# A separate tile for the first output rows, and a recut of a transformer block's head: loads, scalings, the turn of the weight splits

## The chip, the cores and the metric

The kernel runs on one core of one Trainium2 chip. A core has a matrix engine (PE, with its weight loads as PEld), three engines that work on rows (DVE, ACT, POOL), a queue engine that issues most transfers (SP), and 16 DMA engines that carry them. The metric is the device time of one execution in microseconds (us), lower is better; a kernel's time is the median of its runs.

## The reference

One transformer block on 1024 rows of width 1024 in float32: a hybrid attention mixer, attention to a memory of 256 rows, and a feed-forward network of 4096. Each is added to its input, behind a root-mean-square norm with weights:

```python
def _rms_norm(x, g):
    xf = x.astype(jnp.float32)
    y = xf * lax.rsqrt(jnp.mean(xf * xf, axis=-1, keepdims=True) + EPS)
    return (y * g.astype(jnp.float32)).astype(x.dtype)
...
    for l in range(DEPTH):
        x = x + _hybrid_mixer(_rms_norm(x, norm1_g[l]), w_in[l], ..., w_out[l])
        x = x + _memory_xattn(_rms_norm(x, norm2_g[l]), mem, mem_norm_g[l], ..., w_xo[l])
        x = x + _sq_relu_mlp(_rms_norm(x, norm3_g[l]), w_ff_in[l], w_ff_out[l])
```

The mixer projects the normed rows with `w_in` to queries, keys, values and gates, rotates queries and keys by position (tables of cosine and sine), attends in four ways (selected single keys; compressed blocks; selected blocks; a window of 512), and multiplies the joined result with `w_out`.

## The kernel before

**Tiles and parts.** The 1024 rows are eight tiles of 128 (one row per partition). Tiles 0 to 3 are part 0, tiles 4 to 7 part 1. A product that needs full accuracy splits each operand into a rounded half and a remainder (`hi`, `lo`, or `xh`, `xl`) and takes three products.

**The head** (part 0, `project` with `whole` false, lines 467 to 640) runs alone, before any attention. `late["x"]` (line 241) starts the load of tile 0 on SP's queue, `const` (210) the identity matrix. `project` issues the broadcast of the norm weights `gb1` on ACT's queue (474), then alternates weight loads of the first chunk of `w_in` (`wraw`, 274) with the loads of tiles 1 to 3 (440). For each tile `norm_T` (343) squares the row on ACT with its sum, takes the inverse root on DVE and POOL (`rsqrt_of`, 247), scales the row on DVE (348) and calls `to_T` (325): eight transposes on PE in two groups of four, each rounded by ACT (255) and its remainder taken by DVE (256). Between `norm_T` and the products the outer code (1523 to 1536) and `constants` (452) issue the constant loads on SP: tables, norm weights of queries and keys, masks. Part 1's tiles are loaded later, and `norm_ahead` (442) scales them at the end of the head, with a second load of the same norm weights (420, from `gain`). The last work of the head are the query projections, whose results DVE and ACT copy to `st` (500, 502); SP stores them (504).

**Weight splits.** `split_w` (260) rounds on ACT and makes the remainder on POOL or DVE in turn; the turn is `plan["i"]` and the list `PLAN_HEAD` or `PLAN_TAIL`. While attention runs the list has one entry.

**Attention and fill.** `together` runs attention of one tile after another beside fill work: part 1's projection, then `between` (1061) for tiles 0 and 1, `between` for tiles 2 and 3, then the feed-forward network of tiles 0 to 3 (`mlp`). `between` multiplies finished attention rows `o` with `w_out`, adds to x, takes norm 2, and attends to the memory. Its rows `o_of` (line 1076), the residual `x2` and the memory's result all come from the ring `b4` with four buffers in pool `dn`. A buffer is free for a new tile when its last user is done; for `x2` of tiles 0 and 1 that is the store to `x2_dr` (1226). Pool `dn` also has the tiles `xh` and `xl`: `xh` holds norm 2's rows, both are taken by `pre_norms` for norm 3.

**Order.** The code issues work in the order of its generators; a scheduler then orders each engine's instructions and decides when a buffer is reused. Engines run their own instructions in that order and wait for each other on semaphores. SP runs its transfers' issues in order, so one that waits holds back all behind it.

Of the kernel before, what the change touches and what calls it, by code (L numbers as in the profile page):

```python
# [9 lines left out]
F32 = mybir.dt.float32  # L10
# [27 lines left out]
    "p1": {"x4": 5, "st": 2, "relu": 4, "wraw": 4, "whi": 6, "wlo": 6, "c8": 4, "c4": 2, "kraw": 5},  # L38
# [20 lines left out]
def shape_constants():  # L59
# [16 lines left out]
        "c_cos": np.ascontiguousarray(cos.reshape(NT, P, 32).transpose(1, 0, 2)),  # L76
        "c_sin": np.ascontiguousarray(s2.reshape(NT, P, 64).transpose(1, 0, 2)),
        "c_ccos": np.concatenate([c2[end], c2[end]], 0),
        "c_csin": np.concatenate([s2[end], s2[end]], 0),
# [101 lines left out]
def build(nc, tc, I, C, out):  # L181
# [25 lines left out]
    def row(ap):  # L207
        return ap[None, :]
# [32 lines left out]
    late = {"x": ring(p1, "x4", [P, DM])}  # L241
    nc.sync.dma_start(late["x"], I["x"][0, 0:P, :])
    ident = const("c_ident", [P, P])
    mhalf = cst.tile([P, 1], F32, tag="mhalf", name="mhalf")
# [98 lines left out]
    def norm_T(pool, x_t, gb, xs):  # L343
        ss = small(at, "nss", 1)
        xn = ring(pool, "x4", [P, DM])
        s.activation(xn, x_t, AF.Square, accum_out=ss)
        r = rsqrt_of(at, ss, DM, 1, "n")
        v.scalar_tensor_tensor(xn, x_t, r[:, 0:1], gb, op0=ALU.mult, op1=ALU.mult)
        to_T(pool, xn, xs, DM // P)
# [92 lines left out]
    def norm_ahead(pool):  # L442

        gb = gain(pool, W["norm1_g"])
# [7 lines left out]
    def constants(pool):  # L452
# [5 lines left out]
        nc.sync.dma_start(ctab[:, 0, :], C["c_ccos"])  # L458
        nc.sync.dma_start(ctab[:, 1, :], C["c_csin"])
        v.tensor_tensor(ctab[:, 0, :], ctab[:, 0, :], qg[:, 2, :], op=ALU.mult)  # L460
        v.tensor_tensor(ctab[:, 1, :], ctab[:, 1, :], qgs[:, 2, :], op=ALU.mult)
        for h, src in enumerate([W["nsa_kn_g"][1:2], W["nsa_kn_g"][1:2], W["nsa_kn_g"][2:3], W["nsa_kn_g"][2:3],
                                 row(W["dsa_kn_g"]), row(W["idx_k_ln_g"]), row(W["idx_k_ln_b"])]):
            nc.sync.dma_start(kg[:, h, :], src.to_broadcast([P, 64]))
        return pc, kg

    def project(pool, part, late, st):
# [4 lines left out]
        if not whole:  # L472
            gb1 = ring(pool, "x4", [P, DM])
            s.dma_start(gb1, row(W["norm1_g"]).to_broadcast([P, DM]))
# [6 lines left out]
        for t in range(nt):  # L481
            if not whole:
                norm_T(pool, ahead.pop(t), gb1, xt_of(t))
                yield 1.0
# [570 lines left out]
    def between(pool, t0, nt, x2s, keep, res=None, then=None, room=None, pace=None):  # L1055
# [11 lines left out]
        else:  # L1067
# [7 lines left out]
            else:  # L1075
                o_of = [ring(pool, "b4", [P, 8, P]) for t in range(nt)]
# [441 lines left out]
    plan["w"] = PLAN_HEAD  # L1518
# [3 lines left out]
    cos = const("c_cos", [P, NT, 32], at)  # L1522
    sin = const("c_sin", [P, NT, 64], at)
# [54 lines left out]
    plan["w"] = PLAN_TAIL  # L1578
# [40 lines left out]
```

## Time and profile before

| | |
|---|---|
| runs (us) | 1686.76, 1686.9, 1682.57 |
| median | 1686.76 |
| profiled execution: its time / its span | 1684.04 / 1682.0 |
| granted PE clock, mean | 0.994 |
| HBM traffic | 224.40 MB moved, 132 GB/s over the span |

The span is the stretch in which the engines work; the execution's own time is 2.04 us longer. "L348" is line 348 of the kernel before. In a row of the timeline the columns are start, duration, engine, line, operation, output and inputs, and in brackets how long the engine was idle before and what ended that. SPq and ACTq are the issues of DMAs. In a matmul's row, "psD<-whi,xh" names the accumulator and the two operands. A DMA's duration on its queue is that of its issue, not of the transfer.

### The profile page before, as it was taken

What the parts mean: (1) busy time and instruction counts of PE and PEld (TensorE: products, weight loads), DVE (VectorE), ACT (ScalarE), POOL (GpSimd) and SP (SyncE); (2) the same over time, 40 slices, a digit from 0 to 9 for tenths busy, and PEclk for the clock granted to TensorE, in tenths of its full rate; (3) what the DMA queues carried; (4) which work ended last, traced back from release to release, by engine and by line L of the source; (5) the groups of instructions that cost most, each with busy time, mean ns of one, the idle gap of its engine ahead of it and who ended that gap; (6) DMA issues with size and microseconds to landing.
All of it is one profiled execution on the core that took longest, in us unless ns stands there. A gap on an engine that the chain in (4) does not pass through costs nothing.

```text
span 1682.0 us, 29000 instructions
## 1 busy us (share of the span) xinstructions
PE 1605.8 (95%) x9554; PEld 1412.6 (84%) x9554; DVE 1127.2 (67%) x2582; ACT 1111.9 (66%) x2783; POOL 958.4 (57%) x1111
## 2 busy tenths in 40 slices
PE   7998998989999889999999999999998999999998
PEld 6998997868779778888888888888888997887787
DVE  4467678785865983575465755656668657888874
ACT  5455898895698768955799558992565554444443
POOL 2265567573642545778567767572246854555556
PEclk9999999999999999999999999999999999999999
DMA  8975433448266322222222212253367442332254
GB/s 266 298 265 168 164 109 133 126 127 277 88 190 212 105 61 67 73 74 66 81 70 74 74 62 81 64 183 123 98 214 257 150 149 91 101 101 94 89 176 138
DMA packets 186086, 224.40 MB, mean 133 GB/s; under 512 B 25424, under 2 KB 138832, under 8 KB 185936
## 3 DMA queue, kind: packets, MB, share of 16 engines
q1 hardware_dynamic: 177856, 211.54, 39.2%
q0 software_dynamic: 7936, 10.49, 2.3%
q8 instruction: 76, 1.25, 0.3%
q14 instruction: 74, 0.61, 0.1%
q10 hardware_dynamic: 144, 0.52, 0.1%
HBM read 189.20 MB, written 33.29 MB: 132 GB/s over the span
## 4 chain that ended last, share of the span: by engine, by line
PE 37%; DVE 6%; ACT 3%; DMA 2%; issue 2%; POOL 1%; SPq 0%; ACTq 0%; DVEq 0%; POOLq 0%
PE psD L236 16%; PE psS L236 8%; PE psPT L236 4%; PE psM L236 4%; PE psPV L236 2%; PE psPT L832 2%; DVE wlo L269 2%; DMA wraw<-in_w_ff_out_dram 1%; DMA w<-in_w_ff_out_dram 1%; POOL wlo L269 1%; ACT dmask L776 1%; ACT whi L264 1%; ACT S L817 0%; ACT ph L255 0%; DVE P L1450 0%
## 5 line engine op out<-in xcount | busy, mean ns | idle before, releaser
L269 POOL TENSOR_TENSOR wlo<-wraw,whi 128x512 fp32r<-128x512 f32 (+1 forms) x229 | 314.0, 1376 | 205.7 <-ACT whi L264 197.6
L264 ACT ACTIVATE whi<-wraw 128x512 fp32r<-128x512 f32 x329 | 201.0, 626 | 165.6 <-DMA wraw<-in_w_ff_in_dram 37.6
L256 DVE TENSOR_TENSOR pl<-psPT,ph 128x512 fp32r<-128x512 f32 (+1 forms) x232 | 142.0, 620 | 73.4 <-ACT ph L255 72.3
L817 ACT ACTIVATE S<-S,mn 128x128 f32<-128x128 f32 (+7 forms) x192 | 143.0, 746 | 58.5 <-DVE mn L815 58.1
L236 PE MATMUL psD<-whi,h 128*128 128x512 f32 x512 | 176.5, 398 | 1.5 <-POOL h L1363 0.8
L255 ACT ACTIVATE ph<-psPT 128x512 fp32r<-128x512 f32 (+1 forms) x232 | 122.7, 540 | 59.9 <-PE psPT L832 54.0
L822 POOL TENSOR_SCALAR S<-S,sums,gi 128x640 f32<-128x640 f32 (+7 forms) x128 | 113.8, 898 | 82.7 <-DVE sums L820 66.9
L832 PE MATMUL psPT<-c_ident,S 128*128 128x128 f32 x816 | 132.0, 274 | 3.9 <-POOL S L822 1.6
L236 PE MATMUL psD<-wlo,xh 128*128 128x256 f32 (+1 forms) x512 | 131.7, 311 | 0.9 <-POOL wlo L269 0.3
L236 PE MATMUL psD<-whi,xh 128*128 128x256 f32 (+1 forms) x512 | 131.1, 313 | 1.4 <-DMA whi<-W 0.7
L269 DVE TENSOR_TENSOR wlo<-wraw,whi 128x512 fp32r<-128x512 f32 (+1 forms) x100 | 93.3, 938 | 51.0 <-ACT whi L264 49.4
L236 PE MATMUL psS<-K,qh 128*128 128x384 f32 (+3 forms) x288 | 106.3, 372 | 7.3 <-DVE mn L815 5.9
L236 PEld LDWEIGHTS psD<-whi,h 128*128 128x128 f32 x512 | 95.8, 189 | 19.4 <-DVE b L1048 1.4
L832 PEld LDWEIGHTS psPT<-c_ident,S 128*128 128x128 f32 x816 | 97.1, 140 | 13.7 <-POOL S L822 5.0
L236 PE MATMUL psD<-xh,whi 128*128 128x512 f32 (+1 forms) x296 | 103.0, 348 | 0.0
L236 PE MATMUL psD<-xl,whi 128*128 128x512 f32 (+1 forms) x296 | 102.2, 347 | 0.0
L236 PE MATMUL psD<-xh,wlo 128*128 128x512 f32 (+1 forms) x296 | 102.2, 345 | 0.0
L236 PE MATMUL psD<-wlo,h 128*128 128x512 f32 x256 | 101.6, 398 | 0.5 <-POOL wlo L269 0.5
L236 PE MATMUL psS<-K,ql 128*128 128x384 f32 (+3 forms) x288 | 96.3, 338 | 0.8 <-DVE ql L256 0.8
L236 PEld LDWEIGHTS psD<-whi,xh 128*128 128x128 f32 x512 | 92.0, 191 | 5.8 <-DMA whi<-W 1.2
L236 PEld LDWEIGHTS psD<-wlo,xh 128*128 128x128 f32 x512 | 91.8, 191 | 4.1 <-POOL wlo L269 0.5
L776 ACT ACTIVATE dmask<-tkl,tkt 128x384 bf16<-128x384 uint16 (+5 forms) x96 | 84.4, 879 | 7.2 <-DVE tkl L774 5.6
(406 smaller groups left out, 5155.2 us busy)
## 6 DMA issues: line engine op xcount, KB each, us to landing
wraw<-in_w_ff_in_dram SPq DMA_DIRECT2D x44, 512.0 KB, 3.8
wraw<-in_w_ff_in_dram SPq DMA_DIRECT2D x64, 256.0 KB, 2.7
wraw<-in_w_ff_out_dram SPq DMA_DIRECT2D x64, 256.0 KB, 2.7
wraw<-in_w_ff_out_dram SPq DMA_DIRECT2D x24, 512.0 KB, 4.5
w<-in_w_ff_out_dram SPq DMA_DIRECT2D x20, 512.0 KB, 5.7
wlo<-in_w_out_dram SPq DMA_DIRECT2D x36, 256.0 KB, 4.0
whi<-in_w_out_dram SPq DMA_DIRECT2D x36, 256.0 KB, 4.1
wraw<-in_w_in_dram SPq DMA_DIRECT2D x24, 256.0 KB, 5.4
```

The costliest lines, as they stand in the source:

```text
L236: te.matmul(o, a, b, start=start, stop=stop)
L255: late["round"] = s.activation(hi, src, AF.Copy).ins
L256: late["split"] = v.tensor_tensor(lo, src, hi, op=ALU.subtract).ins
L264: s.activation(hi, raw, AF.Copy)
L269: (v if l == "v" else g).tensor_tensor(lo, raw, hi, op=ALU.subtract)
L776: s.activation(mask, src, AF.Sign, bias=c, accum_out=over)
L817: s.activation(S, S, AF.Exp, bias=low, scale=-1.0, accum_out=sums[:, hh:hh + 1])
L822: g.tensor_scalar(Ss[hh], Ss[hh], sums[:, hh:hh + 1], 1.0 if gate is None else gate[:, hh:hh + 1], op0=ALU.mult, op1=ALU.mult)
L832: te.transpose(p2[:, j, hh, :], S[:, (c + j) * P:(c + j + 1) * P], ident)
```

## The change

1. The norm weights are loaded once, into a tile `g` of their own, on SP's queue as third transfer. `norm_T` and `norm_ahead` use it. The load on ACT's queue and the second load go, and the ring `x4` has four buffers instead of five.
2. `norm_T` scales a row in two halves of 512 and transposes each behind its scaling. The square of tile 1 is issued behind the last rounding of tile 0 on ACT (`issue_after`).
3. Cosine and sine come in one tile and load, the compression's two tables too, and the two key norm weights that were loaded twice each come by one load each.
4. The turn of the splits starts at 1 in the head and is set back by one for the tail.
5. The rows `o` of tiles 0 to 3 go to the tile `xl` of pool `dn` instead of the ring `b4`.

```diff
-    "p1": {"x4": 5, "st": 2, "relu": 4, "wraw": 4, "whi": 6, "wlo": 6, "c8": 4, "c4": 2, "kraw": 5},
+    "p1": {"x4": 4, "st": 2, "relu": 4, "wraw": 4, "whi": 6, "wlo": 6, "c8": 4, "c4": 2, "kraw": 5},
...
-        "c_cos": np.ascontiguousarray(cos.reshape(NT, P, 32).transpose(1, 0, 2)),
-        "c_sin": np.ascontiguousarray(s2.reshape(NT, P, 64).transpose(1, 0, 2)),
-        "c_ccos": np.concatenate([c2[end], c2[end]], 0),
-        "c_csin": np.concatenate([s2[end], s2[end]], 0),
+        "c_trig": np.ascontiguousarray(np.concatenate([cos, s2], 1).reshape(NT, P, 96).transpose(1, 0, 2)),
+        "c_ctab": np.tile(np.stack([c2[end], s2[end]], 1), (2, 1, 1)),
...
-    late = {"x": ring(p1, "x4", [P, DM])}
+    late = {"x": ring(p1, "x4", [P, DM]), "g": p1.tile([P, DM], F32, tag="g", name="g")}
     nc.sync.dma_start(late["x"], I["x"][0, 0:P, :])
     ident = const("c_ident", [P, P])
+    nc.sync.dma_start(late["g"], row(W["norm1_g"]).to_broadcast([P, DM]))
...
-    def norm_T(pool, x_t, gb, xs):
+    def norm_T(pool, x_t, gb, xs, after):
         ss = small(at, "nss", 1)
         xn = ring(pool, "x4", [P, DM])
-        s.activation(xn, x_t, AF.Square, accum_out=ss)
+        with tc.issue_after(after) if after else ExitStack():
+            s.activation(xn, x_t, AF.Square, accum_out=ss)
         r = rsqrt_of(at, ss, DM, 1, "n")
-        v.scalar_tensor_tensor(xn, x_t, r[:, 0:1], gb, op0=ALU.mult, op1=ALU.mult)
-        to_T(pool, xn, xs, DM // P)
+        for c in range(0, DM, 512):
+            cs = slice(c, c + 512)
+            v.scalar_tensor_tensor(xn[:, cs], x_t[:, cs], r[:, 0:1], gb[:, cs], op0=ALU.mult, op1=ALU.mult)
+            to_T(pool, xn[:, cs], [x[:, c // P:c // P + 4] for x in xs], 4)
...
-        gb = gain(pool, W["norm1_g"])
+        gb = late["g"]
...
-        nc.sync.dma_start(ctab[:, 0, :], C["c_ccos"])
-        nc.sync.dma_start(ctab[:, 1, :], C["c_csin"])
+        nc.sync.dma_start(ctab, C["c_ctab"])
...
-        for h, src in enumerate([W["nsa_kn_g"][1:2], W["nsa_kn_g"][1:2], W["nsa_kn_g"][2:3], W["nsa_kn_g"][2:3],
-                                 row(W["dsa_kn_g"]), row(W["idx_k_ln_g"]), row(W["idx_k_ln_b"])]):
-            nc.sync.dma_start(kg[:, h, :], src.to_broadcast([P, 64]))
+        for b in range(2):
+            nc.sync.dma_start(kg[:, 2 * b:2 * b + 2, :], W["nsa_kn_g"][None, b + 1:b + 2, :].to_broadcast([P, 2, 64]))
+        for h, src in enumerate([W["dsa_kn_g"], W["idx_k_ln_g"], W["idx_k_ln_b"]], 4):
+            nc.sync.dma_start(kg[:, h, :], row(src).to_broadcast([P, 64]))
...
-            gb1 = ring(pool, "x4", [P, DM])
-            s.dma_start(gb1, row(W["norm1_g"]).to_broadcast([P, DM]))
...
-                norm_T(pool, ahead.pop(t), gb1, xt_of(t))
+                norm_T(pool, ahead.pop(t), late["g"], xt_of(t), late["round"] if t == 1 else None)
...
-                o_of = [ring(pool, "b4", [P, 8, P]) for t in range(nt)]
+                both = pool.tile([P, nt, 8, P], F32, tag="xl", name="xl")
+                o_of = [both[:, t] for t in range(nt)]
...
-    plan["w"] = PLAN_HEAD
+    plan.update(w=PLAN_HEAD, i=1)
...
-    cos = const("c_cos", [P, NT, 32], at)
-    sin = const("c_sin", [P, NT, 64], at)
+    trig = const("c_trig", [P, NT, 96], at)
+    cos, sin = trig[:, :, 0:32], trig[:, :, 32:96]
...
-    plan["w"] = PLAN_TAIL
+    plan.update(w=PLAN_TAIL, i=plan["i"] - 1)
```

At the very start, tile 0's scaling is two rows on DVE now, and the first weight's remainder (POOL's before) stands behind them; tile 1's scaling, which stood between the two remainders of tile 0's transposes, stands behind both. On ACT the square of tile 1 stands behind tile 0's two roundings, where it stood ahead of them.

On SP, the last constants and the first weights behind them (`pc` holds norm weights and tables, `x_281` and `x_283` the masks), before:

```order
L457 DMA pc<-in_dsa_ckv_g_dram 128x128
L458 DMA pc<-in_c_ccos_dram 128x64
L459 DMA pc<-in_c_csin_dram 128x64
L464 DMA pc<-in_nsa_kn_g_dram 128x64
L218 DMA x_281<-in_c_masks_dram 128x640
L464 DMA pc<-in_nsa_kn_g_dram 128x64 x2
L218 DMA x_285<-in_c_cmask_dram 128x512
L464 DMA pc<-in_nsa_kn_g_dram 128x64
L464 DMA pc<-in_dsa_kn_g_dram 128x64
L464 DMA pc<-in_idx_k_ln_g_dram 128x64
L464 DMA pc<-in_idx_k_ln_b_dram 128x64
L274 DMA wraw<-in_w_in_dram 128x2x256
```

and now:

```order
L459 DMA pc<-in_dsa_ckv_g_dram 128x128
L460 DMA pc<-in_c_ctab_dram 128x128
L464 DMA pc<-in_nsa_kn_g_dram 128x2x64 x2
L466 DMA pc<-in_dsa_kn_g_dram 128x64
L216 DMA x_283<-in_c_masks_dram 128x640
L466 DMA pc<-in_idx_k_ln_g_dram 128x64
L466 DMA pc<-in_idx_k_ln_b_dram 128x64
L216 DMA x_287<-in_c_cmask_dram 128x512
L273 DMA wraw<-in_w_in_dram 128x2x256
```

Three loads fewer stand here, and one fewer (cosine and sine) ahead of it; the weights follow the masks directly.

On DVE at the end of the head, before (`S_1562` to `S_1568` are tiles 4 to 7, `x4_1758` the norm weights, `st` the query copies, `K` key remainders):

```order
L500 COPY st_1870<-psD_1863 128x256
L249 TENSOR_SCALAR nms_1779<-nss_1776 128x1
L449 SCALAR_TENSOR_TENSOR S_1562<-S_1562,nr_1765,x4_1758 128x1024
L449 SCALAR_TENSOR_TENSOR S_1564<-S_1564,nr_1781,x4_1758 128x1024
L249 TENSOR_SCALAR nms_1795<-nss_1792 128x1
L500 COPY st_1870<-psD_1880 128x256
L578 TENSOR_TENSOR K_125<-psM_1721,K_125 64x4x128
L249 TENSOR_SCALAR nms_1812<-nss_1809 128x1
L500 COPY st_1910<-psD_1903 128x256
L578 TENSOR_TENSOR K_125<-psM_1728,K_125 64x2x128
L449 SCALAR_TENSOR_TENSOR S_1566<-S_1566,nr_1797,x4_1758 128x1024
L500 COPY st_1910<-psD_1920 128x256
```

and now (`g_76` the norm weights, `S_1558` to `S_1564` tiles 4 to 7):

```order
L451 SCALAR_TENSOR_TENSOR S_1558<-S_1558,nr_1759,g_76 128x1024
L500 COPY st_1864<-psD_1857 128x256
L451 SCALAR_TENSOR_TENSOR S_1560<-S_1560,nr_1775,g_76 128x1024
L248 TENSOR_SCALAR nms_1789<-nss_1786 128x1
L500 COPY st_1864<-psD_1874 128x256
L248 TENSOR_SCALAR nms_1806<-nss_1803 128x1
L578 TENSOR_TENSOR K_127<-psM_1717,K_127 64x4x128
L500 COPY st_1904<-psD_1897 128x256
L578 TENSOR_TENSOR K_127<-psM_1724,K_127 64x2x128
L451 SCALAR_TENSOR_TENSOR S_1562<-S_1562,nr_1791,g_76 128x1024
L451 SCALAR_TENSOR_TENSOR S_1564<-S_1564,nr_1808,g_76 128x1024
L500 COPY st_1904<-psD_1914 128x256
```

The first copy moved behind the first scaling, and the last copy behind the last scaling, which it used to precede.

On SP, about tile 2's output projection in `between`, before (`o_98` and `o_97` are the stored attention rows of tile 2, which L1092 loads; `x_117` and `x_118` are stored residual rows, `b_7280` is x of tile 2, `in_w_out_dram` its weights):

```order
L1226 DMA x_117<-b_5883 128x1024
L315 DMA wlo<-in_w_out_dram 128x2x256
L1085 DMA b_7280<-in_x_dram 128x1024
L315 DMA whi<-in_w_out_dram 128x2x256
L1226 DMA x_118<-b_5884 128x1024
L1092 DMA b_7269<-o_98 128x512
L1092 DMA b_7269<-o_97 128x512
```

and now (the same rows of tile 2 are `o_100` and `o_99`; `in_w_xq_dram` and `in_w_xo_dram` are the weights of the cross-attention of tiles 0 and 1, `oc` its result):

```order
L314 DMA whi<-in_w_xq_dram 128x2x256
L314 DMA wlo<-in_w_xq_dram 128x2x256
L314 DMA whi<-in_w_xq_dram 128x2x256
L1093 DMA xl<-o_100 128x512
L1093 DMA xl<-o_99 128x512
L314 DMA wlo<-in_w_xo_dram 128x2x256
L846 DMA o_102<-oc 64x2x128
```

The rows of tile 2 now come right behind the query weights of tiles 0 and 1 and ahead of `w_xo`, where before they stood behind `w_xo`, the next `w_out` and the stores of tiles 0 and 1. On PE tile 2's output projection therefore starts some 24 rows earlier, ahead of scores that it followed. The order of the engines differs from there to the end of the feed-forward network of tiles 0 to 3; in the tail it is the same.

## The prediction

> **What bounds the kernel now.** I read the totals first, then busy time by stretch, then the stretches that the change touches in order of time, with what ended each wait.
>
> ```profile
> PE 1605.8 (95%) x9554; PEld 1412.6 (84%) x9554; DVE 1127.2 (67%) x2582; ACT 1111.9 (66%) x2783; POOL 958.4 (57%) x1111
> 0.00:20.00 20.00, 9.05 (x51) 8.25 (x52) 9.27 (x16) 10.80 (x19) 4.84 (x10) 1.00 0.69 232
> 20.00:40.00 20.00, 18.53 (x150) 17.55 (x149) 10.21 (x24) 10.01 (x26) 5.27 (x8) 1.00 0.91 299
> 40.00:60.00 20.00, 20.00 (x178) 20.00 (x177) 12.01 (x41) 9.75 (x37) 7.25 (x10) 1.00 1.01 294
> 480.00:500.00 20.00, 17.29 (x106) 15.12 (x104) 14.00 (x42) 19.54 (x55) 9.38 (x15) 1.00 0.62 199
> 500.00:520.00 20.00, 19.79 (x92) 17.34 (x93) 7.43 (x22) 15.21 (x40) 0.26 (x1) 0.91 0.86 269
> 560.00:580.00 20.00, 16.80 (x117) 14.13 (x116) 18.70 (x59) 15.68 (x45) 12.94 (x22) 1.00 0.34 94
> 600.00:800.00 200.00, 193.64 (x1037) 166.04 (x1036) 117.75 (x283) 148.32 (x349) 130.85 (x135) 0.99 0.22 69
> ```
>
> The columns are the stretch, its length, then busy time with instruction counts of PE, PEld, DVE, ACT and POOL, then granted clock, DMA share and GB/s. PE is the bound: it idles 1682.0 - 1605.8 = 76.2 us in all. No matmul is removed, so the change can win only idle time or slow starts. 10.95 us of the idle lies in the first 20 us, 1.47 in the next 20 and none in the third. What PE gains before 40 us is therefore kept at 60 us, if its inputs come earlier too. The chain that ended last does not reach back to the head, so I worked from waits.
>
> **The head: norm weights, halves, constants.**
>
> ```profile
> 0.72 0.41 ACTq L474 DMA_DIRECT2D x<-in_norm_g_dram  x1
> 0.73 0.40 SPq L242 DMA_DIRECT2D x<-in_x_dram  x1
> 6.34 1.06 ACT L346 ACTIVATE x<-x 128x1024 f32<-128x1024 f32 x1 [3.89 <-DMA x<-in_x_dram]
> 7.20 0.47 SPq L212 DMA_DIRECT2D c_cos<-in_c_cos_dram  x1
> 8.28 1.26 POOL L269 TENSOR_TENSOR wlo<-wraw,whi 128x512 fp32r<-128x512 f32 x1
> 8.34 2.28 DVE L348 SCALAR_TENSOR_TENSOR x<-x,nr,x 128x1024 f32<-128x1024 f32 x1 [0.67 <-POOL nr L251]
> 8.61 1.06 ACT L346 ACTIVATE x<-S 128x1024 f32<-128x1024 f32 x1 [0.61 <-DMA S<-in_x_dram]
> 10.68 1.97 PE L335 MATMUL psM<-c_ident,x 128*128 128x128 f32 x8 [10.68 <-DVE nms L249]
> 11.83 0.60 ACT L255 ACTIVATE xh<-psM 128x512 fp32r<-128x512 f32 x1 [2.07 <-PE psM L335]
> 13.06 1.28 DVE L348 SCALAR_TENSOR_TENSOR x<-S,nr,x 128x1024 f32<-128x1024 f32 x1
> 13.58 0.41 PE L236 MATMUL psD<-whi,xh 128*128 128x256 f32 x1
> 16.46 0.28 PE L236 MATMUL psD<-whi,xh 128*128 128x256 f32 x1
> 21.27 0.43 SPq L464 DMA_DIRECT2D pc<-in_idx_k_ln_g_dram  x1
> 21.78 0.40 SPq L464 DMA_DIRECT2D pc<-in_idx_k_ln_b_dram  x1
> 22.75 0.38 SPq L274 DMA_DIRECT2D wraw<-in_w_in_dram  x1
> 26.92 0.63 ACT L264 ACTIVATE whi<-wraw 128x512 fp32r<-128x512 f32 x1 [4.04 <-DMA wraw<-in_w_in_dram]
> 29.30 0.66 PE L535 MATMUL psM<-c_ident,relu 128*128 128x128 f32 x4 [0.57 <-DVE xl L256]
> L358 DVE SCALAR_TENSOR_TENSOR relu<-b,nr,h x22: 734/748/1805, 404.6 to 1300.4; 128x512 f32<-128x512 f32 x22
> ```
>
> First the start. The whole-row scaling takes 2.28 us for tile 0 but 1.28 for tile 1; beside the long one POOL computes a weight remainder (8.28 to 9.54). In the new order this first remainder is DVE's, behind both halves, so the long case goes. A half costs 0.75 (median of the 128x512 row), and PE can begin its transposes 2.28 - 0.75 = 1.53 us earlier. The price is 2 x 0.75 - 1.28 = 0.22 us more DVE per tile, 0.9 for four, beside DMA-bound and PE-bound work.
>
> Moving the weights' broadcast onto SP's queue, third behind x and the identity, delays every later load by one issue (about 0.45). Against this x no longer loads beside another 512 KB issued 0.01 us earlier. The trace does not show x alone: 512 KB at the 299 GB/s of the second stretch is 1.75 us (an estimate), so x lands 0 to 1.75 us earlier. I take 0.9, the middle, since neither end has a nearer row. [...]
>
> But ACT limits the lead. Today it squares tile 1 at 8.61, in the gap of 2.07 us before the first rounding at 11.83. Now that square (1.06) stands behind tile 0's two roundings, by the issue-after. The rounding starts 1.53 + 0.9 = 2.4 us earlier, and 1.06 us of work follows it that used to precede it: the lead that is left is some 1.4, and would be 0.5 if x gained nothing. Matmuls also run slowly at first: the same product takes 0.41 us at 13.58 and 0.28 at 16.46, at granted clock 1.00. [...]
>
> Then SP. Between 7.20 and 21.78 it issues 21 constant loads, and only then, at 22.75, the next chunk's first weights. ACT waits 4.04 us for these with its rounding, and behind that wait stands the last rounding of x, whose remainder PE awaits at 29.30. Seventeen loads remain in that stretch. Late in it SP issues one each 21.78 - 21.27 = 0.5 us, so four fewer are worth 4 x 0.5 = 2.0 us there, and ACT goes on 2.0 us earlier. PE can use this up to its own lead (1.4) plus the 0.57 it waits, about 2.0; the extra DVE work (0.9, partly on the way to that remainder) takes half a microsecond. I take **-1.5 us** for the head. Bounds: -2.4 (the whole early start) to +0.4 (x lands no earlier, and the DVE work takes 0.9 from a lead of 0.5). The ring of scratch rows loses a buffer that the weights held; PE is never idle from 40 to 60 us, so nothing is charged. The split turn changes only which of DVE and POOL makes a remainder; the later turn is restored.
>
> **The second load of the norm weights.**
>
> ```profile
> 116.58 0.37 SPq L420 DMA_DIRECT2D x<-in_norm_g_dram  x1
> 119.24 0.42 DVE L500 COPY st<-psD 128x256 f32<-128x256 f32 x1
> 122.07 2.48 DVE L449 SCALAR_TENSOR_TENSOR S<-S,nr,x 128x1024 f32<-128x1024 f32 x2 [2.35 <-DMA x<-in_norm_g_dram]
> 124.53 0.41 DVE L500 COPY st<-psD 128x256 f32<-128x256 f32 x1
> 125.00 0.38 PE L236 MATMUL psD<-whi,c 128*128 128x256 f32 x1 [0.86 <-DVE st L500]
> 128.22 0.42 DVE L500 COPY st<-psD 128x256 f32<-128x256 f32 x1
> 129.12 2.20 SPq L305 DMA_DIRECT2D whi<-W  x4
> 130.69 0.50 PE L236 MATMUL psD<-w,xh 128*128 128x256 f32 x2 [2.71 <-DVE xl L256]
> 132.66 0.36 PE L236 MATMUL psD<-whi,xh 128*128 128x256 f32 x1 [0.28 <-DMA whi<-W]
> ```
>
> DVE waits 2.35 us for the load that goes. Its rows after that run without a gap, so PE's remainder xl comes up to 1.85 earlier: 2.35 less one copy (0.42) that now stands between the two scalings. What is late next is SP: its weights whi<-W follow the last query store, which needs the copy now placed behind the last scaling. That copy would end at 128.0 instead of 128.64, so the loads start about 0.65 to 1.0 earlier, and PE, which today gets them 0.28 late, then waits for them. I take **-1.0**; bounds -1.85 (loads in time) and +0.5 (the first copy, 119.24, falls behind a scaling and holds PE's bank).
>
> **The rows of tiles 2 and 3.**
>
> ```profile
> 490.25 0.34 SPq L1226 DMA_DIRECT2D x<-b  x1
> 493.86 1.39 SPq L1092 DMA_DIRECT2D b<-o  x2
> 496.07 0.39 PE L236 MATMUL psPV<-pl,Vd 128*128 128x256 f32 x1 [0.60 <-DVE pl L256]
> 497.50 0.62 PE L236 MATMUL psS<-K,iql 128*128 128x384 f32 x2 [0.23 <-DVE iql L256]
> 500.21 1.35 PE L236 MATMUL psD<-wlo,b 128*128 128x256 f32 x4 [2.08 <-DMA b<-o]
> ```
>
> Tile 2's rows load only when a stored residual row (490.25) has left its slot, and PE waits 2.08 us. In a room of their own they load before W_xo's weights, long before use; that wait goes. The projection then moves ahead of scores, by some 24 PE rows, and could also fill the 0.60 and 0.23. I take **-2.1**, bounds -2.9 and +1.3: the stretch 560 to 580 shows 16% idle where no projection covers attention, 500 to 520 1%; some 9 us uncovered at 15% is 1.3. The room is the tile that the third norm takes later, and that norm needs its twin, still held by the second, so no new wait is charged.
>
> **Sum.** -1.5 - 1.0 - 2.1 = -4.6 us, on a profiled execution of 1684.04 (span 1682.0): 1679.4. The runs before scatter from 1682.57 to 1686.9 with a median of 1686.76; the three and the profiled one average 1685.07. I take 1685.07 - 4.6 = **1680.5**.
>
> **Rivals.**
> - *More is filled*: the head keeps 2.4, the second load 1.85, and all 2.9 us at 490 to 500 is used: -7.2, about 1678. For it: PE has nothing idle from 40 to 60 us that could eat the lead. Against: ACT's order and SP's loads.
> - *The front is eaten*: x lands no earlier, and whi<-W limits PE at 132 us as before. Only the room and a little remain: -2, about 1683. For it: DMA share is 0.91 and more from 20 to 60 us, so weights may set the pace.
> - *Attention is starved, slower than before*: with the projection ahead, scores reach DVE and ACT later. These lead at 560 to 580 us (DVE 18.70 of 20), and PE runs dry behind them. PE idles 3.2% from 600 to 800. If the 240 us from 560 on idled 2.5 points more, this costs 6.0, the room's 2.1 is lost, and the sum is -2.5 + 6.0 = +3.5: 1687.5 to 1688.6. It turns the sign from 4.6 us of new idle on, the forecast's whole gain. Against: the second query projection begins at nearly the same place in PE's order (9 rows earlier), so the shift is soon repaid.
>
> **Chances.** Forecast 50%, more filled 18%, front eaten 18%, starved 14%. A measurement of this kernel tells 0.3%, 5.1 us, from no change. The forecast lies just inside: I give 24 of its 50 to faster, 26 to same. More filled is faster; front eaten is same. Starved at its +3.5 is same too, but its price is open upward (another 2.5 points would make it +9.5): 6 of its 14 to same, 8 to slower. Faster 0.42, same 0.50, slower 0.08. The range, 1674.5 to 1687.5, holds the bounds of the three terms (-7.2 to +2.2) but not the worst of starved.
>
> **What would show it.** Tile 0's scaling as two rows of 0.75 us and transposes at 8.5 to 9.2; the first weights after the constants issued near 20.7 and ACT's wait before 26.9 ended near 25; no DVE wait near 120 for norm weights, and PE then waiting for whi<-W; tile 2's projection begun by 490 without a wait for rows. It would be wrong if PE's idle time between 560 and 1000 us changed by more than 2 us, since I charge nothing there, or if the constants were not what holds ACT at 23 to 27 us.

## The result, and the profile after

| | before | changed |
|---|---|---|
| time, median of 6 runs | 1686.83 us (1682.57 to 1688.74) | 1677.16 us (1675.60 to 1680.16) |
| profiled execution (span) | 1684.04 us (1682.0) | 1675.60 us (1673.7) |
| PE busy, PE idle in the span | 1605.8, 76.2 us | 1603.5, 70.2 us |

The ratio is 0.9946, with an interval of 0.9931 to 0.9961: 6.6 to 11.6 us faster. The forecast was 1680.5 (-4.6 us) with a range of 1674.5 to 1687.5, in which the time lies.

The windows view of the changed kernel, in the stretches shown of before, under the page's total for PE (stretch, length, busy time and counts of PE, PEld, DVE, ACT, POOL, granted clock, DMA share, GB/s):

```profile
PE 1603.5 (96%) x9554; PEld 1410.7 (84%) x9554; DVE 1122.1 (67%) x2587; ACT 1112.0 (66%) x2783; POOL 960.2 (57%) x1110
0.00:20.00 20.00, 8.74 (x51) 7.29 (x52) 10.48 (x20) 10.90 (x19) 5.36 (x10) 1.00 0.68 233
20.00:40.00 20.00, 19.50 (x159) 18.65 (x158) 10.78 (x26) 10.46 (x28) 4.16 (x8) 1.00 0.93 306
40.00:60.00 20.00, 19.55 (x170) 19.22 (x169) 10.10 (x41) 8.41 (x33) 7.09 (x10) 1.00 0.89 279
480.00:500.00 20.00, 19.98 (x117) 18.13 (x115) 10.55 (x30) 18.19 (x53) 6.18 (x11) 1.00 0.67 216
500.00:520.00 20.00, 19.62 (x104) 16.75 (x104) 11.32 (x31) 18.51 (x49) 3.98 (x5) 1.00 0.95 298
560.00:580.00 20.00, 17.01 (x109) 13.86 (x109) 16.48 (x48) 16.18 (x42) 14.04 (x24) 1.00 0.44 116
600.00:800.00 200.00, 194.53 (x1052) 166.65 (x1051) 119.41 (x288) 151.33 (x353) 134.68 (x138) 1.00 0.23 70
```

The first 20 us hold as many matmuls as before (51), and PE now idles 0.45 us between 40 and 60 us, where it was always busy. The large gain is at 480 to 500 us (2.71 us of idle time became 0.02); and where before ran at a granted clock of 0.91 from 500 to 520, this one has 1.00. Of the 8.3 us between the two spans only 6.0 are PE's idle time. The rest is the same matmuls running faster, which no term of the forecast contained.

To place it I matched the matmuls of two profiles in their order and read the time between equal ones. The head has run out at 108 us, the second load's place lies between 108 and 145, the room's between 480 and 790 (times of before). Each cell has the time, in it PE's idle time, and how much of it ran at half clock; the first column of numbers is how far a kernel is ahead of the first profile of before at 108 us. The rows below the second are experiments, told further down.

| kernel | ahead at 108 | 108 to 145 | 480 to 790 |
|---|---|---|---|
| before | 0 | 37.0, 6.2, 0 | 310.0, 14.0, 6.8 |
| changed | -0.5 | 34.8, 4.5, 0 | 303.6, 10.6, 0 |
| before again | 1.0 | 38.9, 7.0, 3.4 | 309.3, 13.1, 10.2 |
| changed again | -2.3 | 34.6, 4.5, 0 | 302.4, 9.2, 3.4 |
| room only | 1.0 | 37.1, 5.5, 3.4 | 302.6, 9.4, 3.4 |
| g on ACT | -0.3 | 35.1, 5.1, 0 | 303.5, 10.1, 3.4 |
| room, once | 0.6 | 35.2, 5.2, 0 | 303.7, 10.1, 3.4 |
| room, once, constants | -0.5 | 35.8, 4.6, 3.4 | 302.9, 10.7, 0 |
| room, once, halves | 0.9 | 36.3, 4.0, 6.8 | 304.7, 11.1, 3.4 |
| the same, square free | -1.9 | 36.0, 4.9, 3.4 | 303.4, 10.8, 0 |
| second tile's room | 0.6 | 38.7, 6.2, 3.4 | 308.1, 12.7, 6.8 |
| first tile's room | -1.9 | 37.5, 5.8, 3.4 | 308.4, 11.2, 10.2 |
| changed, casts on POOL | -1.6 | 35.0, 4.7, 0 | 303.4, 10.3, 3.4 |
| room, once, casts on POOL | -2.2 | 35.5, 5.4, 0 | 303.1, 9.4, 3.4 |

**The head of the changed kernel**, by its timeline (start, length, engine or queue, line, operation, idle time before it and what ended that):

```profile
0.73 0.39 SPq L240 DMA_DIRECT2D x<-in_x_dram  x1
1.65 0.42 SPq L242 DMA_DIRECT2D g<-in_norm_g_dram  x1
4.27 1.06 ACT L346 ACTIVATE x<-x 128x1024 f32<-128x1024 f32 x1 [2.26 <-DMA x<-in_x_dram]
7.47 1.41 DVE L350 SCALAR_TENSOR_TENSOR x<-x,nr,g 128x512 f32<-128x512 f32 x2 [1.86 <-DMA g<-in_norm_g_dram]
8.32 1.94 PE L334 MATMUL psM<-c_ident,x 128*128 128x128 f32 x8 [8.32 <-DVE x L350]
15.81 2.43 DVE L350 SCALAR_TENSOR_TENSOR x<-S,nr,g 128x512 f32<-128x512 f32 x2 [0.38 <-POOL nr L250]
16.27 1.43 POOL L268 TENSOR_TENSOR wlo<-wraw,whi 128x512 fp32r<-128x512 f32 x1
18.17 0.68 DVE L255 TENSOR_TENSOR xl<-psM,xh 128x512 fp32r<-128x512 f32 x1
18.90 0.66 PE L334 MATMUL psM<-c_ident,x 128*128 128x128 f32 x4 [1.44 <-DVE xl L255]
20.98 0.43 SPq L273 DMA_DIRECT2D wraw<-in_w_in_dram  x1
21.66 0.60 PE L334 MATMUL psM<-c_ident,x 128*128 128x128 f32 x4
24.76 0.49 DVE L217 CAST c_masks<-x 128x640 bf16<-128x640 f32 x1 [2.26 <-DMA x<-in_c_masks_dram]
26.32 0.63 ACT L263 ACTIVATE whi<-wraw 128x512 fp32r<-128x512 f32 x1 [3.38 <-DMA wraw<-in_w_in_dram]
```

x lands 2.07 us earlier (4.27 against 6.34), but DVE then waits 1.86 us for the norm weights, which stand third on SP's queue. Transposes start at 8.32, 2.36 earlier. At 21.66 they are where they were (21.59): tile 2's scaling takes 2.43 us beside POOL's remainder, and the remainder of x behind it, which PE awaits, is late. The first weights behind the constants are issued 1.8 us earlier (20.98) and land only 0.6 earlier (26.32).

**The second load and the room**, by the timelines of PE and DVE:

```profile
118.78 1.28 DVE L451 SCALAR_TENSOR_TENSOR S<-S,nr,g 128x1024 f32<-128x1024 f32 x1 [0.61 <-POOL nr L250]
...
127.35 0.51 PE L234 MATMUL psD<-w,xh 128*128 128x256 f32 x2 [1.59 <-DVE xl L255]
130.45 0.36 PE L234 MATMUL psD<-whi,xh 128*128 128x256 f32 x1 [1.40 <-DMA whi<-W]
...
491.79 1.03 PE L234 MATMUL psD<-wlo,xl 128*128 128x256 f32 x4
492.66 1.03 PE L234 MATMUL psD<-whi,xl 128*128 128x256 f32 x4
493.52 1.03 PE L234 MATMUL psD<-wlo,xl 128*128 128x256 f32 x4
```

DVE waits for no load there, PE's remainder comes 3.3 us earlier (127.35 against 130.69) and PE then waits 1.40 for whi<-W. Tile 2's projection begins at 491.79 without a wait (the prediction's sign said by 490).

### The profile page after: what moved, and what is told of

The parts are those of the page before. It is cut to its first block, busy times and chain, and to the rows that moved or that the text cites. A ratio compares the mean times of both kernels' runs of the same rounds, so it can differ in the third digit from the quotient of the medians.

```text
span 1673.7 us, 28995 instructions
## 1 busy us (share of the span) xinstructions
PE 1603.5 (96%) x9554; PEld 1410.7 (84%) x9554; DVE 1122.1 (67%) x2587; ACT 1112.0 (66%) x2783; POOL 960.2 (57%) x1110
## 4 chain that ended last, share of the span: by engine, by line
PE 64%; DVE 12%; DMA 8%; ACT 6%; POOL 5%; issue 4%; SPq 1%; ACTq 0%; POOLq 0%; DVEq 0%
PE psD L234 32%; PE psS L234 11%; PE psM L234 6%; PE psPT L234 4%; PE psPV L234 4%; PE psPT L832 4%; DVE wlo L268 2%; POOL wlo L268 2%; DMA wraw<-in_w_in_dram 2%; DVE S L815 1%; DVE pl L255 1%; DMA wraw<-in_w_ff_out_dram 1%; ACT dmask L776 1%; POOL S L822 1%; ACT whi L263 1%
## 5 line engine op out<-in xcount | busy, mean ns | idle before, releaser
L268 DVE TENSOR_TENSOR wlo<-wraw,whi 128x512 fp32r<-128x512 f32 (+2 forms) x101 | 97.7, 975 | 51.0 <-ACT whi L263 48.1
L234 PE MATMUL psD<-whi,xl 128*128 128x256 f32 (+1 forms) x432 | 120.4, 315 | 0.2
```

The source lines that it names most:

```text
L234: te.matmul(o, a, b, start=start, stop=stop)
L268: (v if l == "v" else g).tensor_tensor(lo, raw, hi, op=ALU.subtract)
```

## The experiments

Each was timed in five rounds beside the kernel before, on one chip for each group of four. The theories go by letters. Of the room: A, its order and its waits shorten the middle, against B, the clock fell luckily; later G, tile 2's wait is the core of it, against H, any room does it, and I, the particular order does. Of the head: C, the early start is used up by 22 us, against D, it is kept; E, the merged constants cost by late masks that hold DVE, against F, the halves cost, and J, the weights' transfers set the pace.

**First group: the kernels again, the room alone, the load on the other queue.** Two have no edit. Room only:

```diff
-                o_of = [ring(pool, "b4", [P, 8, P]) for t in range(nt)]
+                both = pool.tile([P, nt, 8, P], F32, tag="xl", name="xl")
+                o_of = [both[:, t] for t in range(nt)]
```

g on ACT, on the changed kernel:

```diff
-    nc.sync.dma_start(late["g"], row(W["norm1_g"]).to_broadcast([P, DM]))
+    s.dma_start(late["g"], row(W["norm1_g"]).to_broadcast([P, DM]))
```

> The kernel before, unchanged, profiled a second time. Open is how much of the 6.4 us that the changed kernel gained between 490 and 780 us (by the place of equal matmuls in the two profiles: lead 1.46 us at 480, 7.9 at 780) is the granted clock: the first profile of before has two stretches of 3.41 us at half clock there, at 501 and 624 us, worth up to 1.7 us each, and the changed kernel has none. Theory A (the room shortens the middle by its order and its waits): the time from 480 to 780 repeats within 1 us in this profile, wherever the half-clock stretches fall. Theory B (chance of the clock): the half-clock stretches fall elsewhere, the middle is some 3 us shorter and another place longer. Time ratio to before: 1.000 by both, interval within 0.2%.

> Before, with the rows of tiles 2 and 3 in the room and nothing else. From 10% of the instructions on, every engine has the order of the changed kernel. Theory A (most of the gain is the room's): ratio 0.9960 (-6.4 us of 1684), lead over before 0 at 480 us and about 6.4 at 800. Theory B (the room is worth its 2.1 us of PE wait at 500, the rest was clock): ratio 0.998 (-3 us), lead 2 to 3 at 800. The prediction's own terms: -2.1 us, ratio 0.9988.

> The changed kernel, unchanged, beside the others on one chip, with a second profile. Ratio 0.9946 as before by both theories (0.993 to 0.996). Against room_only it shows what head and second load give together: theory C (the head's lead is used up by 22 us and only the second load is kept, as the two profiles show: lead 2.4 us at 10 us, -0.07 at 22, -0.5 at 80 to 100, 1.7 at 140): 1.2 to 1.7 us less than room_only. The prediction's terms (head 1.5 and second load 1.0, both kept): 2.5 us less.

> The changed kernel with its one load of the norm weights issued from ACT's queue beside x again, as in before; every engine's order stays as in the changed kernel, except that SP has the load no longer and a few of its rows move. Theory C (the early start is used up by 22 us, because DVE and the weights' transfers set the pace there): x lands about 2 us later, the first transpose starts about 1 us later than 8.3 (the weights no longer hold DVE, x does), and the whole kernel is the same within 0.5 us: ratio to the changed kernel 1.000. Rival D (the start is kept to the end): 1.0 to 2.4 us slower, ratio to the changed kernel 1.001.

| | median, us | ratio to before | interval |
|---|---|---|---|
| before again | 1685.32 | 0.9988 | 0.9975 to 1.0001 |
| room only | 1679.63 | 0.9944 | 0.9923 to 0.9964 |
| changed again | 1674.95 | 0.9924 | 0.9906 to 0.9942 |
| g on ACT | 1675.71 | 0.9929 | 0.9915 to 0.9943 |

The room carries most of the gain. Its stretch takes 309 to 310 us in the old order and 302.4 to 303.6 in the four profiles of the new one: theory A holds for the time. B holds in part: the half-clock stretches do move (in the second profile of before they begin at 572 and 620 us, no longer at 501 and 624), but the old order has them wherever they fall. With the norm weights back beside x, transposes start later (9.06 us, in place of 8.32 and 8.77 in the two profiles of the changed kernel) and the time is the same: the start is not kept (theory C). At 108 us all three profiles of the new head are behind the three of the old one. By the ratios changed again lies 3.4 us below room only, where C expected 1.2 to 1.7 and the prediction's terms 2.5; the intervals overlap, so the times don't decide between these.

What stands ahead of half clock is seen in the windows view of before, cut at the stretches in which the clock was half (columns as above):

```profile
494.14:497.55 3.41, 2.57 (x17) 1.84 (x15) 3.33 (x11) 3.36 (x11) 1.46 (x2) 1.00 0.81 254
497.55:500.97 3.42, 1.34 (x6) 0.94 (x7) 1.74 (x5) 3.33 (x9) 1.73 (x2) 1.00 0.99 352
500.97:504.38 3.41, 3.41 (x10) 2.65 (x9) 0.70 (x2) 2.48 (x8) 0.00 (x0) 0.50 0.81 213
504.38:507.79 3.41, 3.41 (x18) 2.97 (x17) 1.43 (x4) 0.92 (x2) 0.00 (x0) 1.00 0.91 282
...
620.40:623.85 3.45, 1.33 (x5) 0.78 (x5) 3.45 (x10) 2.83 (x9) 0.72 (x1) 1.00 0.00 0
623.85:627.26 3.41, 3.34 (x13) 3.15 (x14) 2.80 (x11) 3.39 (x9) 1.57 (x2) 0.50 0.22 58
```

In the window with the wait of 2.08 us PE is busy 1.34 of 3.42 us; the next 3.41 us run at half clock, with 10 matmuls where the window after has 18. That is 1.7 us more, behind a wait of 2.1. The windows lie on a grid of 3.41 us that differs from run to run: every change of clock in the trace lies a whole number of times 3.413 us behind its first record of the clock, which stands at 16.28 us in before and at 11.62 in the changed kernel. In the fourteen profiles of this study, from 20 us to 7 us before the end and starting at full clock, every one of the 44 windows in which PE was busy less than 45% is followed by half clock, 31 of 98 with 45 to 60%, 7 of 304 with 60 to 80%, and none of 6215 busier ones. (In the last 7 us nine of ten below 45% are, one at 44% is not.) Such a window need not be idle: PE was busy 0.39 of it in the two shown, ahead of 501 and of 624 us.

The same is seen, less clearly, where the second load was waited for. The old head has idle time of 5.5 to 7.0 us between 108 and 145, and a half-clock stretch there in four of its five profiles that keep that load, against three of the nine profiles without it.

**Second group: the second load, the constants, the halves, each on top of the room.** From about 90 us on all four have the changed kernel's order on PE up to short pieces. Once (the first load stays on ACT's queue, into the tile `g`; the ring `x4` has four buffers, as in the change):

```diff
-        gb = gain(pool, W["norm1_g"])
+        gb = late["g"]
...
-            gb1 = ring(pool, "x4", [P, DM])
-            s.dma_start(gb1, row(W["norm1_g"]).to_broadcast([P, DM]))
+            gb1 = late["g"]
+            s.dma_start(gb1, row(W["norm1_g"]).to_broadcast([P, DM]))
```

Constants adds the merged tables and key gains of the change; halves adds its loop over half rows with the square behind the roundings; the last leaves the square free:

```diff
-        with tc.issue_after(after) if after else ExitStack():
-            s.activation(xn, x_t, AF.Square, accum_out=ss)
+        s.activation(xn, x_t, AF.Square, accum_out=ss)
```

> Room only, and the norm weights loaded once, from ACT's queue beside x as in before, into a tile of their own; rows whole, constants as in before. Theory E (the second load gives its part, and the rest of the head gives nothing or costs): lead over before (first profile, equal matmuls) about 0.7 at 104 us, as in the two other profiles of the old head (1.03 and 0.99), about 2.8 at 140, and the whole 2 us less than room_only, so as fast as the changed kernel or up to 1 us faster. Rival (the head gives 1.5 as predicted): 1.5 us slower than the changed kernel. The prediction's size of the second load: 1.0 less than room_only.

> room_once with the constants merged (four loads fewer ahead of the weights), nothing else. Theory E (the merging costs: the scheduler now places the masks behind the key gains, they land 2 to 4 us later than 22.7 us, as in the three profiles of the changed head, the vector engine's casts and the remainder behind them come late, and PE waits): first wait of DVE for c_masks ends at 24.5 to 26.5, lead over before at 104 us 0.6 to 1.5 less than room_once's. Rival F (merging is harmless or worth the predicted 2.0 at SP; the halves cost): masks by 23, lead at 104 us no less than room_once's, or up to 2 more.

> room_once with the scaling in halves and tile 1's square behind tile 0's roundings, nothing else (constants and split turn as in before). Theory E: x lands beside the norm weights as in before, so transposes start some 1.5 us earlier than 10.7; masks at 22.7 as in before; lead over before at 104 us like room_once's (within 0.7), the early start being used up by the weights' transfers. Rival F (the halves cost, by two instructions in place of one on DVE and the later square): 0.6 to 1.5 less lead than room_once at 104 us. Rival D (the early start is kept where constants don't spoil it): 1 to 1.5 more.

> room_once with the scaling in halves, tile 1's square left where the scheduler puts it (ahead of tile 0's roundings). The prediction's step (the square behind the roundings is what lets the early start through; ahead of them it would delay the first rounding by up to 1.06): first rounding of x 0.5 to 1.06 us later than in room_once_halves. At 104 us no difference above 0.7 by theory E, since the lead is used up before; 1 less by rival D.

| | median, us | ratio to before | interval |
|---|---|---|---|
| room, once | 1675.94 | 0.9934 | 0.9914 to 0.9954 |
| room, once, constants | 1675.07 | 0.9933 | 0.9913 to 0.9952 |
| room, once, halves | 1675.67 | 0.9939 | 0.9921 to 0.9957 |
| room, once, halves, square free | 1677.04 | 0.9947 | 0.9929 to 0.9965 |

The times can't be told apart, nor from the changed kernel. Room and one load, with the old head, are enough for all of its gain. The interval of room only (0.9923 to 0.9964) doesn't lie apart from these either, so what the second load adds is read from profiles alone. The profiles say more. The second load's place shortens from 37.1 us (room only) to 35.2. With the constants merged the kernel is 1.1 us less far ahead at 108 us than without (-0.5 against 0.6), with halves it is 0.2 further; one profile each, where profiles of one head differ by about 1 us. The last profile has a half-clock stretch of 6.8 us at 25 us, worth up to 3.4 us, so its -1.9 can't be put down to the square. What was expected of it, a first rounding 0.5 to 1.06 us later than with halves alone, did not come: that rounding begins at 9.93 us in both, since the free square runs from 8.60 to 9.66, in time in which ACT otherwise waits for PE.

Why merging the constants doesn't pay is in SP's issues and ACT's wait for the weights. Room, once:

```profile
18.67 0.35 SPq L218 DMA_DIRECT2D x<-in_c_masks_dram  x1
23.21 0.38 SPq L274 DMA_DIRECT2D wraw<-in_w_in_dram  x1
26.82 0.63 ACT L264 ACTIVATE whi<-wraw 128x512 fp32r<-128x512 f32 x1 [4.21 <-DMA wraw<-in_w_in_dram]
```

and with the constants merged:

```profile
19.22 0.35 SPq L216 DMA_DIRECT2D x<-in_c_masks_dram  x1
21.10 0.38 SPq L272 DMA_DIRECT2D wraw<-in_w_in_dram  x1
24.72 0.49 DVE L217 CAST c_masks<-x 128x640 bf16<-128x640 f32 x1 [2.74 <-DMA x<-in_c_masks_dram]
26.57 0.63 ACT L262 ACTIVATE whi<-wraw 128x512 fp32r<-128x512 f32 x1 [4.00 <-DMA wraw<-in_w_in_dram]
```

The weights are issued 2.1 us earlier and land 0.25 earlier. Over all profiles ACT's wait ends at 26.3, 28.0, 26.7, 26.6 and 27.2 us with merged constants (mean 27.0) and at 26.1 to 28.5 in the nine others (mean 26.9). On the mean nothing is won: the issues came earlier and the landings did not, so the time is set behind the issue. From issue to ACT's start the weights took 3.6 us in room, once, and 5.5 with the constants merged, 4.2 in before and 5.3 in the changed kernel, in the last two at a DMA share of 0.78 and 0.77; what made the way longer is not shown. The masks, now behind three of the five loads of key gains, land at 24.7 to 26.5 us where the old head has them at 22.4 to 23.2.

**Third group: which part of the room, and the masks.** On before, the room for the second tile of each pair, or (the line behind the dots, in place of the one above it) for the first:

```diff
-                o_of = [ring(pool, "b4", [P, 8, P]) for t in range(nt)]
+                both = pool.tile([P, nt, 8, P], F32, tag="xl", name="xl")
+                o_of = [both[:, t] if t else ring(pool, "b4", [P, 8, P]) for t in range(nt)]
...
+                o_of = [both[:, 0] if t == 0 else ring(pool, "b4", [P, 8, P]) for t in range(nt)]
```

On the changed kernel, and on room with one load, the casts:

```diff
-        v.tensor_copy(t, f)
+        nc.gpsimd.tensor_copy(t, f)
```

> Before, with only the second tile of each pair (tiles 1 and 3) in the room; tile 2's rows stay in the ring. DVE, ACT and POOL keep the order of before entirely, PE too, SP moves the load of tile 3 by a few rows. The stretch between the matmuls at 480 and 790 us of before took 310.0 and 309.3 us in two profiles of the old order and 302.4 to 304.7 in eight of the new. Theory G (the gain is tile 2's: its wait of 2 us, the half-clock stretch that follows a 3.4 us window in which PE was busy less than about 45%, and what the earlier projection fills behind it): the wait for b<-o near 500 stays, the stretch takes 308 to 310, ratio 0.999 to 1.000. Rival H (any room in the ring gives it, by freeing slots for what follows): 303 to 305, ratio 0.996.

> Before, with only the first tile of each pair (tiles 0 and 2) in the room; the order from 480 us on is a third one, neither before's nor the changed kernel's. Theory G: PE's wait for tile 2's rows goes, and most of the gain comes with it whatever the order behind: the stretch of 480 to 790 takes 303 to 306 us, ratio 0.996 to 0.998, and the half-clock stretch near 501 is gone. Rival I (the particular order of the changed kernel gives what exceeds the wait): 307 to 308, the wait's 2.1 us alone, ratio 0.9988.

> The changed kernel with the two casts of the masks on POOL (idle there) in place of DVE; the order differs only in the first 5% of the instructions. Theory E (the late masks hold DVE, behind whose casts the remainder of x stands that PE awaits at 26 to 30 us): DVE's remainder no longer stands behind a cast, and the lead at 108 us over the first profile of before is about 0.7, as in the old head, in place of -0.5, -2.3 and -0.3 in the three profiles of the new one: 1 to 1.7 us faster than the changed kernel. Rival J (the weights' transfers set the pace there and the masks only come beside it): lead stays at -0.3 to -1.0.

> Room, norm weights loaded once, old head, and the masks' casts on POOL: the candidate for a faster version than the changed kernel. Theory E: masks were no obstacle in the old head (22.7 us), so the lead at 108 us stays at about 0.6 (room_once) and the time that of room_once: 1670 to 1676, ratio 0.992 to 0.994. Rival: another 0.5 to 1 us at 108 us, since DVE waits 1.3 to 2.0 us for the masks in the old head too.

| | median, us | ratio to before | interval |
|---|---|---|---|
| second tile's room | 1685.19 | 0.9996 | 0.9987 to 1.0005 |
| first tile's room | 1683.67 | 0.9982 | 0.9968 to 0.9997 |
| changed, casts on POOL | 1677.01 | 0.9950 | 0.9936 to 0.9963 |
| room, once, casts on POOL | 1679.04 | 0.9964 | 0.9950 to 0.9978 |

The second tile's room gives nothing, and the wait for tile 2's rows stays, by PE's timeline, with half the clock behind it (cut near its own grid, hence 0.54):

```profile
500.50:503.90 3.40, 1.20 (x6) 0.86 (x5) 1.59 (x4) 3.31 (x9) 1.74 (x2) 1.00 0.96 347
502.96 1.13 PE L236 MATMUL psD<-wlo,b 128*128 128x256 f32 x4 [2.20 <-DMA b<-o]
503.90:507.30 3.40, 3.40 (x10) 2.69 (x10) 0.86 (x2) 2.31 (x8) 0.00 (x0) 0.54 0.67 170
```

So rival H falls. With the first tile in the room that wait is gone (PE busy 20.00 of 20 from 480 to 500), but by the windows view the half clock comes three times further on (0.91, 0.95 and 0.88 below):

```profile
480.00:500.00 20.00, 20.00 (x122) 18.30 (x121) 12.20 (x33) 19.35 (x54) 6.74 (x12) 1.00 0.60 181
560.00:580.00 20.00, 17.23 (x108) 14.45 (x106) 17.54 (x58) 15.14 (x45) 13.28 (x22) 0.91 0.25 72
600.00:620.00 20.00, 17.97 (x105) 16.25 (x104) 17.38 (x41) 14.51 (x33) 6.94 (x7) 0.95 0.28 84
620.00:640.00 20.00, 18.88 (x98) 15.59 (x96) 12.60 (x34) 18.18 (x46) 7.71 (x10) 0.88 0.05 14
```

Its idle time from 480 to 790 is 11.2 us, 2.1 less than the mean of the three profiles in before's order (13.3), which is the wait's size. The time is only 0.7 less (308.4 against 309.1), since 10.2 us of it ran at half clock. By the ratio the kernel is 3.0 us faster than before (0.5 to 5.4), and room only is 9.5 faster (6.1 to 13.0). Rival I is nearer than theory G: with the wait gone, but another order behind it, some 2 to 3 us are won, and the rest of the room's gain needs the whole room. That the order behind the wait gives this rest is argued, not shown: the profile is the slowest of this kernel's eleven runs (1688.59 against a median of 1683.67), so its three half-clock stretches may be chance.

The casts on POOL free DVE, as expected, and don't help:

```profile
25.65 0.72 POOL L217 CAST c_masks<-x 128x640 bf16<-128x640 f32 x1 [8.80 <-DMA x<-in_c_masks_dram]
27.18 0.63 ACT L263 ACTIVATE whi<-wraw 128x512 fp32r<-128x512 f32 x1 [5.08 <-DMA wraw<-in_w_in_dram]
28.95 0.65 PE L535 MATMUL psM<-c_ident,relu 128*128 128x128 f32 x4 [1.93 <-ACT pe L1501]
```

That is the changed kernel with POOL's casts: no remainder waits for a cast, ACT still waits for the weights to 27.18, and at 108 us the kernel is 1.6 behind before. Theory E's mechanism falls; rival J (the transfers set the pace) stands, though its lead of -0.3 to -1.0 was too hopeful. On the old head the move is no gain either: the 1679.04 lies above the 1670 to 1676 expected, and the profile's lead is -2.2 in place of 0.6. There ACT has its weights at 28.45, the latest of all profiles, PE waits 3.05 us until 30.83 for the remainder behind them, and 3.4 us at half clock follow. No variant beats the changed kernel beyond the intervals.

## Why the prediction was right, and where not

The direction held and the time lies in the range, but two of the three terms were mis-sized by a factor of 2.5 or more, and the third had the wrong sign; the errors partly cancel. Some of it was luck: the gain, 9.1 us by the ratio, is twice the 4.6 of the forecast and more than the 7.2 that the bounds of its terms allow, but before's median, 1686.83, lies 1.8 above the 1685.07 from which the forecast was taken, and so the time still fell in the range. The interval is clear of no change; the chances had given 0.50 to a time that can't be told from before's, and 0.42 to faster. By stretches of the table:

| term | forecast | measured |
|---|---|---|
| head | -1.5 | +1.2 |
| second load | -1.0 | -2.5 |
| rows of tiles 2, 3 | -2.1 | -5.8 |

Head: lead at 108 us, mean of the six profiles with the old head 0.2, of the three with the new one -1.0 (those with halves or constants alone or casts on POOL left out). One of the six (first tile's room) has 3.4 us at half clock at 24 us; without it the old head's mean is 0.7. Both scatter by about 1 us, so the loss is likely, its size rough. Second load: mean of five profiles with it 37.8 us, of nine without 35.4. Room: 309.1 (three in before's order) against 303.3 (ten).

**Head.** Six steps:
- *x lands 0 to 1.75 us earlier, taken 0.9.* It was 2.07, over the bound, and transposes started at 8.32, ahead of the 8.5 to 9.2 of the signs (8.77 in the second profile). The middle was my estimate for want of a nearer row, and the far end came. I didn't price that the norm weights, third on SP, become the next wait (1.86 us of DVE).
- *The long case goes, since the first remainder is DVE's.* It moved: tile 2's scaling now meets POOL's remainder and takes 2.43 us in place of 1.41. Its first half takes 0.75 us; the second starts at 16.49, 0.22 behind that remainder, and takes 1.76. In before the whole row took 2.28 us, started 0.06 behind a remainder of 1.26 on POOL, and 1.28 with none beside it. In these rows the one that started second was the longer: in the profiles of the second and of the first tile's room, with before's head, the scaling starts at 7.9, ahead of POOL, and takes 1.28; POOL's remainder then takes 2.15 and 2.29, and transposes start at 9.2 in place of 10.4 to 10.7. So the 1.53 us were read from a start that does not always fall that way.
- *ACT limits the lead, so the square goes behind the roundings.* With the old loads the first rounding begins at 9.93 whether the square stands ahead or behind; in the changed kernel this was not tried apart.
- *Matmuls run slowly at first, at granted clock 1.00.* The 1.00 was misread. The trace's first record of the clock is at 16.28 us in before and at 11.62 in the changed kernel, and the view prints 1.00 where it has none. Eight transposes take 1.97 us at 10.68 and 1.17 at 18.32 (from start to start 0.213 us and 0.109), and the change of pace falls on that first record in the profiles. Over the fourteen profiles the slow phase lasts 3.3 to 6.6 us from the first matmul, and it is 5.6 in this one of before and 3.3 in this one of the changed kernel: part of its early lead is the place of the grid.
- *Four loads fewer at SP put ACT's wait 2.0 earlier.* This is the step that failed. The issue came at 20.98, close to the 20.7 of the signs, and the wait ended at 26.32, not near 25. I read a time of issue as a time of landing, and the way between them grew from 4.2 to 5.3 us (DMA's share in it 0.78 and 0.77, from 20 to 40 us 0.91 and 0.93); the rival "front is eaten" had it.
- *PE is never idle from 40 to 60, so what is gained is kept.* True of before, but the gain was gone at 21.66 us already, and the new head idles 0.45 between 40 and 60.

**Second load.** The mechanism was right, down to the next wait (PE for whi<-W, 1.40). Idle time fell by 1.35 (6.12 to 4.77 on the mean), near the forecast. Some 0.6 more is half clock (2.7 us of it in a profile with the load, 1.5 without, at half effect); the remaining half a microsecond I can't place.

**Room.** The wait, 2.08 us, went, and with the first tile's room idle time falls by about that much. What the term left out is twofold: the half-clock stretch that followed the wait (3.41 us, from 500.97), and, it seems, the order of scores and projections from there on, which I took for neutral. Idle time fell by 3.1 us (13.3 to 10.2), half clock from 8.0 to 2.4 us a profile, worth 2.8. I had noted slow matmuls at the start of the kernel, and not asked the same of a wait in the middle.

**Rivals.** "More filled" came nearest in time (1678), though not by its mechanism: it counted on a head that gains 2.4, and on no more than 2.9 us for the room. "Attention is starved" fell: with 580 to 600 and 800 to 1000 beside the rows above, PE's idle time between 560 and 1000 us went from 11.5 to 9.2. By my own sign (more than 2 us there) the forecast of no effect behind the projection was wrong, to the good side.

**Open.** The three measured terms make -7.1; the ratios say 9 for the changed kernel and 13 for its second series. The half-clock stretches from 1260 us on move by several microseconds between profiles of one order (400.0 and 398.7 us in two of before for the same matmuls to 1660, 396.4 to 402.5 in those with the room), and may hold the rest; that wasn't separated. Nor was it tried whether another order behind the room would do better.

## What to carry to other kernels

Price a wait of PE by the window it falls in: in these runs, where PE was busy less than 45% of a window of 3.41 us, half clock followed (44 of 44), which by my estimate cost up to 1.7 us more for each 3.41 us of it (10 matmuls, where the window after had 18), so the wait of 2.08 us cost nearly 4. Removing it is not sure to win that much, as the first tile's room shows, where half clock came elsewhere. An earlier issue need not land earlier: here the weights were issued 1.8 us earlier and landed 0.6 earlier (2.1 and 0.25 on the old head). Look first at what the issue's way to the landing took before. And a change that lets a scheduler reorder should be read as two changes, the wait that goes and the order that comes; a variant that has the one without the other helps to tell them apart, and it needs more than one profile.

## What the runs showed of the hardware that was not expected

- The clock fell to half also behind windows that were not idle: 44 of 44 windows of 3.41 us with PE busy below 45% (0.39 ahead of 501 us in before), 31 of 98 between 45 and 60%, none of 6215 above 80%. The grid's place differs between profiles of one kernel: from 128.00 to 131.43 PE is busy 0.74 us in the first profile of before and 0.72 in the second, and what follows runs at 1.00 in the one and at 0.50 in the other.

```profile
128.00:131.43 3.43, 0.74 (x6) 0.74 (x7) 3.33 (x10) 0.97 (x3) 0.00 (x0) 1.00 0.55 181
131.43:134.84 3.41, 3.02 (x23) 2.54 (x22) 1.44 (x4) 0.60 (x1) 2.63 (x4) 1.00 1.02 336
```

```profile
128.00:131.43 3.43, 0.72 (x7) 0.48 (x6) 3.33 (x10) 1.23 (x3) 0.00 (x0) 1.00 0.49 156
131.43:134.84 3.41, 3.41 (x19) 3.41 (x18) 0.99 (x3) 0.22 (x1) 2.63 (x4) 0.50 0.97 311
```

- Of two loads of 512 KB that start together on two queues, x was there some 1.4 to 2.1 us later than when it was issued alone ahead of the other: at 5.88 to 6.34 us in eleven profiles, against 4.26 to 4.47 in three.
- At the start PE ran at about half its pace (transposes start 0.213 us apart, later 0.109; products 0.213, later 0.120) for 3.3 to 6.6 us from its first matmul, while the windows view shows a clock of 1.00 for want of a record.
